# A chunked recurrence on one Trainium2 core: small work moved off VectorE, and a new trace order for output work, late values and the first group's tail

## The chip, the cores and the metric

One core of a Trainium2 chip runs the program. Five engines work beside each other, each on its own stream of instructions: TensorE (PE in the profile, with its weight loads as PEld), VectorE (DVE), ScalarE (ACT), GpSimd (POOL) and SyncE (SP), which here only issues DMAs, in the order of its stream. The metric is the device time of one execution in microseconds; lower is better.

## The reference

One step of a two-layer model: an RWKV-7 time mix with its feed-forward net (FFN), then a latent attention layer with its FFN. Prompt: 512 tokens behind 16 meta tokens; beside it 8 sequences of 4 new tokens, so 560 rows of width 1024. The part that this change touches is the recurrence, for each of 16 heads of width 64, cut from the reference:

```python
def step(s, inp):                       # s: value x key, one per head
    r_t, d_t, k_t, v_t, kk_t, ka_t = inp
    sa = einsum('bhvk,bhk->bhv', s, kk_t)
    s = s * d_t - sa[..., None] * ka_t + v_t[..., None] * k_t
    return s, einsum('bhvk,bhk->bhv', s, r_t)
...
o = groupnorm(o) * lnx_g + lnx_b + bonus * v     # per head
x = x + (o * g) @ wo                             # then x = x + sqrelu_mlp(rmsnorm(x))
```

The 8 new sequences start from states of their own.

## The kernel before

Matrices are fp32 products made from high and low parts in three passes (L326, L337); the low part of a weight, `wlo`, is a subtraction of 128x1024 elements on VectorE (L308), of some late weights on GpSimd.

The recurrence runs in chunks. The 528 prompt rows are 8 chunks of 64 tokens and a tail of 16, to which the 32 rows of the new sequences are added. In a chunk a head needs a unit triangular inverse T of 64x64, the products with the state, and the state's update. The heads are in two groups of four pairs, `st` = 0 and 1; each chunk is worked in two halves of two pairs.

- `inverse(st)`: 31 steps of a multiply and a subtract on VectorE (L637, L638) make the 32x32 inverses; they go to DRAM (`X_D` at L640, a transposed copy `XT_D` at L643). `inverse_tail` does the same in 15 steps for the tail's 16x16 blocks (L660, L661, store L663, loads into `TTt` L667).
- `merge(st)` loads the blocks (L816, L817, L824) and makes 64x64 inverses from them on PE (L839, L847).
- `chunk` (L882 on for its solve): PE multiplies with the chunk's inputs (L886); ScalarE copies the result (`rb`, L888); PE applies T (L892); two evacuations write the solved rows into `SUV`, one by ScalarE (L894), one by the engine that `VA` names for the group (L893); PE makes the state's increment (L912); GpSimd scales the old state (`SL`, L330); VectorE adds both into the next chunk's `SUV` (L920) and again into the next state `Sp` (L922); PE makes the chunk's output (L928, L932).
- `out(p, a, b)` (L1083 on) is one output step for pairs p, p+1 and the rows a to b: means on PE (L1095), centring on VectorE (L1097), squares on ScalarE (L1098), variances on PE (L1102), Ln and Exp on ScalarE (L1103, L1104), scale and bonus on VectorE (L1106, L1107), the gate's product on PE (L1113) with its weights `lg` loaded through a ring of two (L1112), then L1114 and the split in high and low. `wo0` and `wo1` multiply by `wo` and add x; `late_ffn` runs the first 256 rows through the first quarters of the FFN.
- `tail(st)` works the tail chunk, `states(st)` makes the final states: GpSimd masks (`uvm`) and scales (`Sn`) 128x576 elements, PE multiplies (L1042, L1043), VectorE adds.
- `v_late` computes the second group's values, adds them to the bonus (`z`, L1196, stored at L1197) and transposes them into `V_D` (L601 on PE).

What sets the order: `rwkv()` has these as flows, named I (inverse and merge of group 1), J (inverse of the tail), C (chunks of group 0), Y (`v_late`), Oa and Ob (output steps of group 0, first 256 rows and the other 304), L and M (tails of group 0 and 1), W (`wo0`), S and Q (states), D (chunks of group 1), Pa and Pb (output steps of group 1), Xa and Xb (`wo1`), F (`late_ffn`). Each has a list of what must be done before it, and an entry in `PLAN` of a start and a step. A loop takes the flow with the smallest due time among those that may go, runs one piece and adds its step. The order of this trace is a priority for the scheduler that places the instructions on each engine. Needs that matter here: Oa needs C's pieces up to 21 (half of its chunks), L needs C and J, Ob needs L, D needs I and Y, Pa needs D's pieces up to 21 and Ob, M needs D and J, Pb needs M and Pa, F needs Xa, Xb needs Pb and F.

Of the kernel before, what the change touches and what calls it, by code (L numbers as in the profile page):

```python
# [19 lines left out]
D = 1024  # L20
# [12 lines left out]
C = 64  # L33
# [172 lines left out]
class Kern:  # L206
# [3 lines left out]
    ORDER = ["B0 P R D-1 C0 P A1 P E0 P"] * NP  # L210
    WL, ON_V = [1, 4, 6, 8], ((0, 1, 2, 3), (0, 1))
    AMIX, LOP = {4: (0, 1, 2, 3, 4, 5, 6, 7), 5: (0, 1, 2, 3, 4, 5, 6)}, {0: (), 2: (7,)}
    JP, VA, NQ = False, (False, True), (False, False)
    STILL, UNTIL, LATE_LO = (), "I", True
    ON_P, CL = 2, 7
    RA, S0R, MT, VL = 1, True, False, (False, False)
    NPUMP = [0, 0, 0, 2, 4, 4, 4, 4]
    PLAN = dict(I=(0, 1), J=(5.2, 3), C=(6.4, 0.7), Y=(0, 2), Oa=(61, 1.5), L=(72, 1), Ob=(36.5, 0.231), W=(72, 1),
                S=(88.5, 7.65), D=(39, 1), Pa=(74.5, 1), Xa=(70, 0.357), F=(70.5, 0.85), M=(80.5, 0.708), Pb=(85, 1.152), Q=(91.5, 2.309), Xb=(80, 1.7))

    def __init__(self, tc, I, O):
        self.tc, self.nc, self.I, self.O = tc, tc.nc, I, O
# [187 lines left out]
    def rwkv(self):  # L410
        nc, tc, I, O, dr = self.nc, self.tc, self.I, self.O, self.dr
# [4 lines left out]
        halves = (slice(0, 64), slice(64, 128))  # L416
# [46 lines left out]
        V = [self.a(f"V{p}") for p in range(NP // 2)]  # L463
        spans = (slice(0, TA), slice(TA, T))
        for s in spans:
            q = self.sm()
# [105 lines left out]
        for k in range(KT):  # L572
            l = l1[k // 4][:, k % 4, :]
            st = dict(start=(k == 0), stop=(k == KT - 1))
            fw, fa, fg = lm[k]
            for h in range(2):
                hs = slice(h * TH, (h + 1) * TH)
# [276 lines left out]
        def pk(q, n):  # L854
            return q[:, 0:64 * n].rearrange("p (a n) -> p a n", n=64)

        def load_chunk(st, c):
            d = ch[st][c] = {"S": [None, None]}
            ps = slice(4 * st, 4 * st + 4)
            if c < 8:  # L860
                d["W"] = tuple(self.xr(f"W{st}_{c}{i}", [128, 4, 128]) for i in range(2))
                d["V"] = v = self.xr(f"SUV{st}_{c}", [128, 4, 2, 64])
                d["AK"] = self.xr(f"AKc{st}_{c}", [128, 8, 64])
                d["R"] = self.ring("r", f"R{st}_{c}", [128, 4, 64], NP)
            else:
                d["W"] = tuple(self.a(f"Wt{st}{i}", [128, 4, 128]) for i in range(2))
                d["V"] = v = self.a(f"SUVt{st}", [128, 4, 2, 64])
                d["AK"] = self.a(f"AKt{st}", [128, 8, 64])
                d["R"] = self.a(f"Rt{st}", [128, 4, 64])
            for i in range(2):  # L870
                gate[st, c] = nc.sync.dma_start(d["W"][i], W_D[c, :, 8 * st + 4 * i:8 * st + 4 * i + 4, :])
            if self.VL[st]:
                nc.sync.dma_start(v, V_D[c, :, ps, :].unsqueeze(2).to_broadcast([128, 4, 2, 64]))
            else:
                nc.sync.dma_start(v[64:128, :, 0, :], V_D[c, 64:128, ps, :])
                nc.sync.dma_start(v[0:64, :, 1, :], V_D[c, 0:64, ps, :])
            nc.sync.dma_start(d["AK"], AK_D[c, :, 8 * st:8 * st + 8, :])
            nc.sync.dma_start(d["R"], R_D[c, :, ps, :])
# [19 lines left out]
        def alternate(inner, outer, prs):  # L898

            for i, pr in enumerate(prs):  # L900
                first, second = (outer, inner) if i % 2 else (inner, outer)
                first(i, pr, True)
                second(i, pr, False)

        def chunk(st, c, hf):
            d = ch[st][c]
            W, V, AK, R = (d[k] for k in ("W", "V", "AK", "R"))
            Sp = d["S"][hf]
            heads, vs = yield from solve(st, W, V, lambda pr: TT[st][pr][:, c, :], [2 * hf, 2 * hf + 1])
            q = self.sm()  # L910
            for i, pr, par in heads:
                nc.tensor.matmul(q[halves[par], i * 64:i * 64 + 64], AK[:, 2 * pr + par, :], V[:, pr, par, :], start=True, stop=True)  # L912
            SL = self.s("SL")
            p0 = 4 * st + 2 * hf
            self.pmul(SL, Sp, LE[:, p0:p0 + 2, c:c + 1].to_broadcast([128, 2, 64]))
            nxt = ch[st][c + 1]
            if c < 7:
                for par in range(2):
                    hs = halves[par]
                    nc.vector.tensor_add(nxt["V"][hs, vs, par, :], pk(q, 2)[hs], SL[hs])  # L920
            nxt["S"][hf] = self.s("Sp")
            nc.vector.tensor_add(nxt["S"][hf], pk(q, 2), SL)  # L922
            yield
            q = self.sm()

            def inner(i, pr, first):
                for par in range(2):
                    nc.tensor.matmul(q[halves[par], i * 64:i * 64 + 64], V[:, pr, par, :], W[pr // 2][:, 2 * (pr % 2) + par, 64:128], start=first, stop=not first)  # L928

            def outer(i, pr, first):  # L930
                for par in range(2):
                    nc.tensor.matmul(q[halves[par], i * 64:i * 64 + 64], Sp[halves[par], i, :], R[halves[par], pr, :], start=first, stop=not first)  # L932
            alternate(inner, outer, [2 * hf, 2 * hf + 1])
            o = 64 * (c % 4)
            nc.scalar.copy(Of[p0, TA * (c // 4)][:, :, o:o + 64], pk(q, 2))
            yield

        def chunks(st):
# [3 lines left out]
            for hf in range(2):  # L942
                d["S"][hf] = self.s("Sp")
                nc.gpsimd.memset(d["S"][hf], 0.0)
            for par in range(2):
# [112 lines left out]
        nxt = dict(R=self.RA)  # L1058
# [113 lines left out]
        def run(*gens):  # L1172
            for g in gens:
                yield from g
# [26 lines left out]
        def late_ffn():  # L1201
            self.stat_seg(0, TA)
            for q in range(self.EARLY):
                yield from self.ffn_seg(q, 0, TA)
# [3 lines left out]
            I=(run(inverse(1), merge(1)), ()),  # L1208
            J=(inverse_tail(), ()),
            C=(c0, ()),  # L1210
            Y=(v_late(), ()),
            Oa=(run(out(0, 0, TA), out(2, 0, TA)), (("C", 21),)),
            L=(tail(0), ("C", "J")),
            Ob=(run(out(0, TA, T), out(2, TA, T)), ("L",)),
            W=(wo0(), ("Oa", "Ob", "Y", ("D", 1))),
            S=(states(0), ("L",)),
            D=(chunks(1), ("I", "Y")),
            Pa=(run(out(4, 0, TA), out(6, 0, TA)), (("D", 21), "Ob")),
            Xa=(wo1(0, TA), ("Pa", "W")),
            F=(late_ffn(), ("Xa",)),  # L1220
            M=(tail(1), ("D", "J")),
            Pb=(run(out(4, TA, T), out(6, TA, T)), ("M", "Pa")),
            Q=(states(1), ("M",)),
            Xb=(wo1(TA, T), ("Pb", "F")))
        done = {n: 0 for n in flows}
        at = {n: self.PLAN[n][0] for n in flows}
        free, now = set(), 0
# [3 lines left out]
        while flows:  # L1231
# [7 lines left out]
            try:  # L1239
                next(flows[n][0])  # L1240
                done[n] += 1
                at[n] += self.PLAN[n][1]
            except StopIteration:
# [680 lines left out]
```

## Time and profile before

| | us |
|---|---|
| median of 3 runs | 1704.0 (1700.67 to 1707.35) |
| profiled execution | 1705.09, its span 1703.3 |
| PE busy in the span | 1575.3 (92%), mean granted clock 0.952 |
| VectorE busy | 972.1 (57%) |
| ScalarE busy | 667.0 (39%) |
| GpSimd busy | 348.4 (20%) |

The span runs from the first instruction to the last. A busy PE still loses time where its granted clock is below 1.00. The stage that the change concerns runs from about 339 us, where the second group's inverse, the first group's chunks and the late values start together, to about 720 us, where the FFN goes on with all rows.

### The profile page before, as it was taken

The page shows a single profiled execution, that of the slowest core. Times are in us where ns is not written, and L with a number is a line of the kernel's source. Part 1 is how long each engine was busy: PE and PEld are TensorE (multiplying, and loading weights), DVE is VectorE, ACT ScalarE, POOL GpSimd, SP SyncE. Part 2 cuts the span into 40 slices and gives each one's busy share as a digit, 9 for nine tenths or more (in the row PEclk, how much of TensorE's full clock was granted, in tenths as well). Part 3 has the DMA queues.
Part 4 walks back from the last instruction along what each step waited for, and adds up shares of the span by engine and source line. Part 5 has one row for each costly group of instructions (what it writes and reads, how often), then busy time and mean ns, then how long its engine had stood idle before and what let it go on. Part 6 is the DMA issues. An engine that isn't in the chain of part 4 may idle for free.

```text
span 1703.3 us, 33334 instructions
## 1 busy us (share of the span) xinstructions
PE 1575.3 (92%) x13474; PEld 1442.5 (85%) x13474; DVE 972.1 (57%) x1601; ACT 667.0 (39%) x1236; POOL 348.4 (20%) x467
## 2 busy tenths in 40 slices
PE   7699897798899997999999999899999999999996
PEld 6478786686689886999999998767679999999996
DVE  6775678465466677555444656555635444444456
ACT  4374545333445443443331442344534331322222
POOL 3623525442111123000000012773500000000000
PEclk9889897698899998999999999999999999999998
DMA  6334556977834454454232243787612222222223
GB/s 206 128 94 129 181 148 189 256 219 191 241 117 156 158 184 140 137 156 129 87 100 78 86 145 117 230 284 222 190 51 81 91 90 87 88 87 87 87 88 102
DMA packets 156475, 240.04 MB, mean 141 GB/s; under 512 B 68417, under 2 KB 100082, under 8 KB 156322
## 3 DMA queue, kind: packets, MB, share of 16 engines
q1 hardware_dynamic: 140466, 189.59, 36.9%
q0 software_dynamic: 15280, 47.59, 8.5%
q8 instruction: 106, 1.74, 0.4%
q10 hardware_dynamic: 576, 0.74, 0.1%
q14 instruction: 47, 0.39, 0.1%
HBM read 200.50 MB, written 37.37 MB: 140 GB/s over the span
## 4 chain that ended last, share of the span: by engine, by line
PE 54%; DVE 2%; ACT 2%; DMA 1%; issue 1%; SPq 1%; POOL 0%; DVEq 0%; ACTq 0%; POOLq 0%
PE mm L326 31%; PE mm L337 12%; PE sm L337 2%; PE sm L1749 2%; PE sm L1656 1%; PE sm L1700 1%; ACT whi L307 1%; PE sm L1602 1%; DMA lN<-latN,idx 1%; PE sm L1640 0%; DVE wlo L308 0%; PE sm L1703 0%; DMA raw<-wall 0%; DVE y L1861 0%; PE mm L1616 0%
## 5 line engine op out<-in xcount | busy, mean ns | idle before, releaser
L307 ACT CAST whi<-raw 128x1024 fp32r<-128x1024 f32 x218 | 228.8, 1050 | 639.7 <-PE mm L326 356.9
L308 DVE TENSOR_TENSOR wlo<-raw,whi 128x1024 fp32r<-128x1024 f32 x214 | 267.4, 1250 | 280.1 <-ACT whi L307 278.2
L337 PE MATMUL mm<-xs,whi 128*128 128x256 f32 (+1 forms) x1024 | 201.0, 294 | 1.4 <-DVE fd L1316 0.9
L337 PEld LDWEIGHTS mm<-xs,whi 128*128 128x128 f32 x1024 | 163.9, 190 | 2.6 <-issue 1.4
L337 PE MATMUL mm<-xs,wlo 128*128 128x256 f32 (+1 forms) x512 | 149.9, 293 | 0.0
L326 PE MATMUL mm<-hh,wlo 128*128 128x272 f32 (+1 forms) x640 | 133.5, 290 | 0.0
L326 PE MATMUL mm<-hl,whi 128*128 128x272 f32 (+1 forms) x640 | 133.4, 290 | 0.0
L326 PE MATMUL mm<-hh,whi 128*128 128x272 f32 (+1 forms) x640 | 133.3, 290 | 0.0
L326 PE MATMUL mm<-h_ffn,whi 128*128 128x272 f32 x512 | 106.2, 289 | 0.5 <-ACT fr L1350 0.5
L326 PE MATMUL mm<-l_ffn,whi 128*128 128x272 f32 x512 | 105.8, 288 | 0.0
L326 PE MATMUL mm<-h_ffn,wlo 128*128 128x272 f32 x512 | 105.4, 287 | 0.0
L326 PEld LDWEIGHTS mm<-hh,whi 128*128 128x128 f32 x640 | 101.1, 188 | 0.0
L326 PEld LDWEIGHTS mm<-hh,wlo 128*128 128x128 f32 x640 | 100.9, 188 | 0.0
L326 PEld LDWEIGHTS mm<-hl,whi 128*128 128x128 f32 x640 | 100.7, 188 | 0.0
L337 PEld LDWEIGHTS mm<-xs,wlo 128*128 128x128 f32 x512 | 97.1, 190 | 0.1
L1859 POOL TENSOR_TENSOR y<-x,rstd 128x272 f32<-128x272 f32 x4 | 3.5, 895 | 456.6 <-DVE wlo L308 449.7
L337 PE MATMUL mm<-hh,wlo 128*128 128x256 f32 (+1 forms) x256 | 76.2, 298 | 5.0 <-DVE wlo L308 5.0
L326 PEld LDWEIGHTS mm<-h_ffn,whi 128*128 128x128 f32 x512 | 79.9, 188 | 1.0 <-ACT fr L1350 1.0
L326 PEld LDWEIGHTS mm<-l_ffn,whi 128*128 128x128 f32 x512 | 80.2, 188 | 0.0
L326 PEld LDWEIGHTS mm<-h_ffn,wlo 128*128 128x128 f32 x512 | 80.1, 188 | 0.0
L337 PE MATMUL mm<-hl,whi 128*128 128x256 f32 (+1 forms) x256 | 75.8, 296 | 3.0 <-DVE hl L1308 3.0
L337 PE MATMUL mm<-hh,whi 128*128 128x256 f32 (+1 forms) x256 | 76.5, 299 | 0.1
(472 smaller groups left out, 3824.3 us busy)
## 6 DMA issues: line engine op xcount, KB each, us to landing
raw<-wall SPq DMA_DIRECT2D x222, 512.0 KB, 3.6
lT<-latT SPq DMA_DIRECT2D x80, 160.0 KB, 3.6
W_D<-sc POOLq DMA_DIRECT2D x16, 512.0 KB, 3.8
W<-W_D SPq DMA_DIRECT2D x32, 256.0 KB, 4.7
AK_D<-akt SPq DMA_DIRECT2D x8, 576.0 KB, 4.6
s<-state SPq DMA_DIRECT2D x16, 256.0 KB, 3.2
AKc<-AK_D SPq DMA_DIRECT2D x16, 256.0 KB, 4.3
V_D<-vt POOLq DMA_DIRECT2D x8, 288.0 KB, 6.3
```

Source lines behind the costliest of these rows:

```text
L307: nc.scalar.copy(hi, raw)
L308: self.lo_on.tensor_sub(lo, raw, hi.bitcast(F32))
L326: nc.tensor.matmul(v[:, h, :], wt[:, k, :], xt[:, off + h * n: off + (h + 1) * n], start=(first and k == 0 and e == 0), stop=(last and k = ...
L337: self.nc.tensor.matmul(v, wt[:, k, :], xt, start=(k == 0 and e == 0), stop=(k == len(xs) - 1 and e == 2))
L1602: nc.tensor.matmul(o, l[:, k0:k0 + kw], w[:, 2 + k, :], start=(k == 0 and e == 0), stop=(k == 1 and e == 2))
L1656: nc.tensor.matmul(q[:, q0:], V[h // 2][b][:, 128 * (h % 2):128 * (h % 2) + 128], PT[b] if b else Pm[h % 2], start=(b == 0), stop=(b == 4))
L1700: nc.tensor.matmul(q[32 * bb:32 * bb + 32, cols], qlT[:, r, 4 * g + bb, :], lt[bb][:, :, 128 * r + 64 * k:128 * r + 64 * k + 64], start=(r ...
L1749: nc.tensor.matmul(qa[rs, 0:RANK], PT[jp // 2][:, o:o + 32], nat[bb][:, RANK * k:RANK * k + RANK], start=(jp == 0 and k == 0), stop=False)
L1859: nc.gpsimd.tensor_mul(y[:, i], x[m][:, s], r)
```

## The change

Four things. The tail's inverse `J` is computed on GpSimd (`JP`). The first group's solved rows are evacuated by ScalarE twice, the second group's by ScalarE and VectorE (`VA`). For the first group the next state `Sp` is no longer added by VectorE; GpSimd copies it in two halves from the next chunk's `SUV`, which holds the same sum (`SP_P`). And `PLAN` has other numbers. The lines below the edited function stand 6 further down afterwards.

```diff
@@ -210,13 +210,14 @@
     ORDER = ["B0 P R D-1 C0 P A1 P E0 P"] * NP
     WL, ON_V = [1, 4, 6, 8], ((0, 1, 2, 3), (0, 1))
     AMIX, LOP = {4: (0, 1, 2, 3, 4, 5, 6, 7), 5: (0, 1, 2, 3, 4, 5, 6)}, {0: (), 2: (7,)}
-    JP, VA, NQ = False, (False, True), (False, False)
+    JP, VA, NQ = True, (True, False), (False, False)
+    SP_P = (True, False)
     STILL, UNTIL, LATE_LO = (), "I", True
     ON_P, CL = 2, 7
     RA, S0R, MT, VL = 1, True, False, (False, False)
     NPUMP = [0, 0, 0, 2, 4, 4, 4, 4]
-    PLAN = dict(I=(0, 1), J=(5.2, 3), C=(6.4, 0.7), Y=(0, 2), Oa=(61, 1.5), L=(72, 1), Ob=(36.5, 0.231), W=(72, 1),
-                S=(88.5, 7.65), D=(39, 1), Pa=(74.5, 1), Xa=(70, 0.357), F=(70.5, 0.85), M=(80.5, 0.708), Pb=(85, 1.152), Q=(91.5, 2.309), Xb=(80, 1.7))
+    PLAN = dict(I=(0, 1), J=(0, 1), C=(6.4, 0.7), Y=(0, 1.3), Oa=(33, 1.5), L=(36, 1), Ob=(36.5, 0.5), W=(42, 2),
+                S=(78.5, 7.65), D=(38, 1), Pa=(64.5, 1), Xa=(70, 0.357), F=(70.5, 0.85), M=(72.5, 0.708), Pb=(85, 1.152), Q=(91.5, 2.309), Xb=(80, 1.7))
 
     def __init__(self, tc, I, O):
         self.tc, self.nc, self.I, self.O = tc, tc.nc, I, O
@@ -914,13 +915,18 @@
             p0 = 4 * st + 2 * hf
             self.pmul(SL, Sp, LE[:, p0:p0 + 2, c:c + 1].to_broadcast([128, 2, 64]))
             nxt = ch[st][c + 1]
+            nxt["S"][hf] = self.s("Sp")
             if c < 7:
                 for par in range(2):
                     hs = halves[par]
                     nc.vector.tensor_add(nxt["V"][hs, vs, par, :], pk(q, 2)[hs], SL[hs])
-            nxt["S"][hf] = self.s("Sp")
-            nc.vector.tensor_add(nxt["S"][hf], pk(q, 2), SL)
-            yield
+            if c < 7 and self.SP_P[st]:
+                for par in range(2):
+                    hs = halves[par]
+                    nc.gpsimd.tensor_copy(nxt["S"][hf][hs], nxt["V"][hs, vs, par, :])
+            yield
+            if c == 7 or not self.SP_P[st]:
+                nc.vector.tensor_add(nxt["S"][hf], pk(q, 2), SL)
             q = self.sm()
 
             def inner(i, pr, first):
```

With the new numbers the trace has `Y` done before the last chunks of `C`, `Oa` and `L` around the end of `C` instead of behind `D`, `Ob` and `W` beside `D`, `Pa` and `Xa` earlier, and `Pb` behind the last piece of `F`, where it had been between the pieces.

SP, where the loads for the second group's chunks are issued, before: behind the merge's loads (`TT`) stand the bonus load and store (`z`, L1193, L1197), the tail inverse's store and loads (L663, L667), then the first chunk's `SUV`.

```order
L824 DMA TT_4303<-X_D_120 32x8x32 x4
L1193 DMA z_4581<-BV_D 128x560
L878 DMA R_3_4823<-R_D 128x256
L1197 DMA BV_D<-z_4581 128x560
L1090 DMA bv_0_4807<-BV_D 128x256
L1090 DMA bv_0_4808<-BV_D 128x256
L663 DMA X_D<-X_3364 48x256
L1090 DMA bv_0_4922<-BV_D 128x256
L1090 DMA bv_0_4923<-BV_D 128x256
L667 DMA TTt<-X_D 16x8x16 x4
L875 DMA SUV_0_4619<-V_D 64x4x64
```

The same place afterwards:

```order
L825 DMA TT_4436<-X_D_120 32x8x32 x4
L1096 DMA bv_0_4473<-BV_D 128x256
L1096 DMA bv_0_4474<-BV_D 128x256
L876 DMA SUV_0_4731<-V_D 64x4x64
L877 DMA SUV_0_4731<-V_D 64x4x64
L878 DMA AKc_0_4732<-AK_D 128x512
L872 DMA W_10_4740<-W_D 128x512
L872 DMA W_11_4741<-W_D 128x512
L876 DMA SUV_1_4742<-V_D 64x4x64
L877 DMA SUV_1_4742<-V_D 64x4x64
L878 DMA AKc_1_4743<-AK_D 128x512
L1118 DMA lg_0_4810<-lorag 128x128
```

The bonus's and the tail inverse's DMAs are gone from between the merge's loads and the first `SUV`; the gate's weights for an output step now follow the second chunk's loads.

PE at the start of the second group's chunks, before: the late values' last transposes (L601), one output step, the first chunk.

```order
L601 MATMUL sm<-cst,V_4580 128x128 x8
L601 MATMUL sm<-cst,V_4580 64x128
L1102 MATMUL mm<-sqo,cst 128x256 x2
L1113 MATMUL mm<-hg,lg_0_4890 128x256
L1113 MATMUL mm<-hg,lg_0_4893 128x256
L1095 MATMUL mm<-Of_0_3407,cst 128x256 x2
L886 MATMUL sm<-SUV_0_4619,W_00_4617 64x64
L886 MATMUL sm<-SUV_0_4619,W_01_4618 64x64
L886 MATMUL sm<-SUV_0_4619,W_00_4617 64x64 x3
L886 MATMUL sm<-SUV_0_4619,W_01_4618 64x64 x3
L892 MATMUL sm<-rb,TT_4300 64x64 x2
L892 MATMUL sm<-rb,TT_4301 64x64 x2
```

Afterwards (L1005 and L1108 to L1119 are the tail and the second output step, then the tail's and the first chunk's solves):

```order
L1005 MATMUL sm<-QRt,Sp 64x32 x8
L1108 MATMUL mm<-sqo,cst 128x256 x2
L1119 MATMUL mm<-hg,lg_0_4810 128x256
L1119 MATMUL mm<-hg,lg_0_4813 128x256
L887 MATMUL sm<-SUVt_4375,Wt_4373 64x64
L887 MATMUL sm<-SUVt_4375,Wt_4374 64x64
L887 MATMUL sm<-SUVt_4375,Wt_4373 64x64 x3
L887 MATMUL sm<-SUVt_4375,Wt_4374 64x64 x3
L893 MATMUL sm<-rb,TTt 64x64 x8
L887 MATMUL sm<-SUV_0_4731,W_00_4729 64x64 x4
L887 MATMUL sm<-SUV_0_4731,W_01_4730 64x64 x4
L893 MATMUL sm<-rb,TT_4433 64x64 x2
```

The transposes are no longer there; the tail of the first group and the second output step stand ahead of the first chunk.

PE at the last output steps of the second group, before, with the matmuls of the FFN piece (L337) around them:

```order
L337 MATMUL mm<-hh,whi_6999 128x256
L337 MATMUL mm<-hl,whi_6999 128x256
L337 MATMUL mm<-hh,wlo_7000 128x256
L1102 MATMUL mm<-sqo,cst 128x304 x2
L337 MATMUL mm<-hh,whi_7029 128x256
L337 MATMUL mm<-hl,whi_7029 128x256
L337 MATMUL mm<-hh,wlo_7030 128x256
L337 MATMUL mm<-hh,whi_7029 128x256
```

Afterwards, behind the last matmul of the FFN pieces (row one):

```order
L338 MATMUL mm<-hh,wlo_7109 128x256
L1108 MATMUL mm<-sqo,cst 128x304 x2
L1119 MATMUL mm<-hg,lg_256_7210 128x304
L1119 MATMUL mm<-hg,lg_256_7213 128x304
L1048 MATMUL sm<-uvm,AKt_4376 64x512
L1049 MATMUL sm<-uvm,AKt_4376 64x64
L1048 MATMUL sm<-uvm,AKt_4376 64x512
L1049 MATMUL sm<-uvm,AKt_4376 64x64
L1101 MATMUL mm<-Of_4_5461,cst 128x304 x2
L1108 MATMUL mm<-sqo,cst 128x304 x2
L1119 MATMUL mm<-hg,lg_256_7244 128x304
L1119 MATMUL mm<-hg,lg_256_7247 128x304
```

Two output steps and the states' matmuls (L1048, L1049) now follow each other with no FFN matmul between them.

## Rows read from the trace of the kernel before

**Rows 1.** Windows; columns: stretch, length, busy us of PE, PEld, DVE, ACT, POOL, clock, DMA.

```profile
339.00:408.30 69.30, 67.20 (x908) 56.55 (x906) 50.23 (x151) 25.54 (x78) 28.99 (x52) 1.00 0.79 228
408.30:438.30 30.00, 19.77 (x323) 15.75 (x323) 9.76 (x28) 10.19 (x26) 4.05 (x11) 0.66 0.61 140
438.30:461.00 22.70, 19.41 (x382) 16.25 (x382) 12.85 (x44) 11.54 (x40) 3.37 (x8) 0.92 0.94 257
461.00:530.00 69.00, 67.16 (x652) 57.62 (x650) 45.29 (x101) 32.41 (x73) 6.99 (x14) 1.00 0.46 146
530.00:641.90 111.90, 109.84 (x891) 99.79 (x892) 76.51 (x98) 49.03 (x67) 25.83 (x30) 1.00 0.52 168
641.90:652.30 10.40, 5.37 (x28) 5.16 (x27) 6.61 (x5) 1.05 (x1) 3.51 (x4) 0.67 0.38 118
652.30:676.30 24.00, 18.87 (x120) 15.35 (x118) 21.53 (x36) 11.68 (x21) 7.06 (x8) 0.98 0.46 147
```

**Rows 2.** Timeline of PE; columns: start, length, engine, line, operation, [idle before <-releaser].

```profile
412.46 0.24 PE L839 MATMUL sm<-xt,n 32*32 32x32 f32 x2 [4.20 <-DMA xt<-XT_D]
440.41 0.64 PE L886 MATMUL sm<-SUV,W 128*64 128x64 f32 x16
444.50 0.64 PE L886 MATMUL sm<-SUV,W 128*64 128x64 f32 x16
452.20 1.13 PE L1113 MATMUL mm<-hg,lg 128*128 128x256 f32 x4 [2.05 <-DMA lg<-lorag]
647.23 0.58 PE L337 MATMUL mm<-hh,wlo 128*128 128x256 f32 x1 [5.03 <-DVE wlo L308]
```

**Rows 3.** Timeline of SP's DMA queue, 413 to 433 us.

```profile
413.17 8.03 SPq L824 DMA_DIRECT2D TT<-X_D  x14
425.28 0.32 SPq L1197 DMA_DIRECT2D BV_D<-z  x1
428.37 0.33 SPq L663 DMA_DIRECT2D X_D<-X  x1
432.20 0.59 SPq L875 DMA_DIRECT2D SUV<-V_D  x1
```

**Rows 4.** Groups by line, 330 to 640 us: count | busy, mean ns | idle before.

```profile
L922 DVE TENSOR_TENSOR Sp<-sm,SL 128x128 f32<-128x128 f32 x32 | 9.3, 291 | 2.8 <-PE sm L912 2.2
L893 DVE TENSOR_SCALAR SUV<-sm 64x128 f32<-64x128 f32 x16 | 4.4, 279 | 5.1 <-PE sm L892 5.1
L661 DVE TENSOR_TENSOR X<-X,itmp 48x15 f32<-48x15 f32 (+7 forms) x15 | 3.7, 247 | 0.2
L990 POOL COPY Wt<-SQ 64x64 f32<-64x64 f32 x8 | 2.6, 320 | 22.7 <-DMA Wt<-W_D 20.9 <-DMA AKt<-AK_D 1.7
```

**Rows 5.** Timeline of POOL and DVE, where both read SBUF.

```profile
371.84 2.36 POOL L308 TENSOR_TENSOR wlo<-raw,whi 128x1024 fp32r<-128x1024 f32 x1
364.29 0.42 DVE L638 TENSOR_TENSOR X<-X,itmp 128x247 f32<-128x247 f32 x1
371.94 2.54 DVE L638 TENSOR_TENSOR X<-X,itmp 128x247 f32<-128x247 f32 x1
640.47 5.56 DVE L1318 TENSOR_TENSOR x<-x,fd 128x256 f32<-128x256 f32 x2
667.28 3.72 DVE L308 TENSOR_TENSOR wlo<-raw,whi 128x1024 fp32r<-128x1024 f32 x1
```

**Rows 6.** Groups by line and shape, 330 to 680 us: output step, states.

```profile
L1102 PE MATMUL mm<-sqo,cst 128*128 128x304 f32 x16 | 5.0, 432 | 0.0
L1103 ACT ACTIVATE sqo<-mm,eps 128x608 f32<-128x608 f32 x4 | 3.1, 769 | 1.5 <-PE mm L1102 1.4
L1106 DVE SCALAR_TENSOR_TENSOR cen<-cen,vecs,sqo 128x304 f32<-128x304 f32 x8 | 3.9, 530 | 4.3 <-ACT sqo L1104 4.3
L1114 DVE TENSOR_TENSOR cen<-mm,cen 128x608 f32<-128x608 f32 x4 | 3.1, 784 | 0.1
L330 POOL TENSOR_TENSOR uvm<-SUVt,cst 128x576 f32<-128x576 f32 x16 | 19.6, 1248 | 34.3 <-DVE x L1318 27.8 <-issue 4.9 <-PE sm L1023 1.6
```

## Prediction

> **What bounds the kernel now.** I read the windows of the stage first, one for each change in what runs [rows 1]: a stretch's length less PE's busy time times the granted clock is what PE loses there, by idling or at the lower clock. A change that leaves PE's instructions as they are (this one does) can only win back such loss, or add to it. In order the seven stretches lose 2.1, 16.95, 4.84, 1.84, 2.06, 6.8 and 5.5 us, 40.1 in all. In the first, where the first group's chunks, the second inverse and the late values run together, VectorE is busy 50.23 of 69.3 us, but PE 67.20 at full clock: PE is the bound. The big hole is 408.3 to 461, with 21.8 us: the end of the inverse, its merge and the start of the second group's chunks. The next are 641.9 to 652.3 and the stretch behind it, 12.3 us.
>
> Then the timelines say what ends the waits. In the hole PE first waits 4.20 us for the transposed inverse, later 2.05 us for gate weights [rows 2]. On SP's queue the merge's fourteen loads end at 413.17 + 8.03 = 421.2; the store of `z` goes at 425.28, the tail inverse's store at 428.37, and only at 432.20 the first load of `SUV` for the second group [rows 3]. The two in between wait for VectorE's results, and everything behind them on SP waits too. At 647.23 PE has idled 5.03 us for a VectorE split [rows 2], which stood behind two additions that took 5.56 us together beside GpSimd's `uvm` [rows 5, 6].
>
> The mean granted clock of 0.66 and 0.67 in the two holes (2.4 GHz is 1.00, the lower level 1.2 GHz) follows the idling there, and is 1.00 in the dense stretches [rows 1].
>
> **The change, part by part.** The sum is made against the profiled execution: 1705.1 us, its span 1703.3 and 1.8 around it. That is 1.1 above the median of three, 1704.0, well inside their spread.
>
> *Tail inverse, copies, evacuations.* VectorE loses 30 operations of the tail inverse (its subtractions 247 ns [rows 4]; the multiplies I take at 0.2 to 0.25), 14 state additions of 291 ns and, in the first group, 16 evacuations of 279 ns [rows 4]: 7 + 4.1 + 4.5, about 15 us. The evacuations come back to VectorE in the second group, where it is busy 45.29 of 69.0 us [rows 1] while PE is full; ScalarE has the same count. GpSimd gains 30 operations and 28 copies; the nearest row is its copy of 64x64, 320 ns [rows 4], so 58 x 0.32 = 18.6 us on top of 28.99 in 69.3 [rows 1], which fits. The cover for all of it is PE, busy 67.2 of 69.3 us. The late values' last transposes, about 2.6 us of PE work that filled part of the hole before, now lie in this stretch: its end moves back by that and the 4.20 us wait shrinks by as much, so that is nil too. For the inverse, the true start of the hole, 15 us less beside it would be a gain, and GpSimd's reads beside it a loss. Between an inverse earlier by the 2.1 us that PE loses there and one later by 6 (below) I take 0.
>
> Here rule and row bear on a loss. The same subtraction of 128x247 took 0.42 us alone and 2.54 while GpSimd made a `wlo` of 2.36 us beside it [rows 5]. The Trainium skill, "SBUF — State Buffer", section "Who interferes with whom", says that a VectorE instruction with two inputs in SBUF and a GpSimd instruction that reads SBUF share a port pair, and whichever comes second is blocked until the first ends. The trace agrees. By that rule in full each of the 58 new GpSimd operations would hold back an inverse step, which is the fourth case below; by the row of the first window alone the cost is nil.
>
> *The hole.* Two trace edits act here. The late values and the tail's inverse end early, so their DMAs no longer stand between the merge's loads and `SUV`: the first `SUV` load can go at about 422, 10 us earlier. But PE is not simply 10 us earlier, because its order now has the second output step and the tail's solve ahead of the first chunk, and that output step's gate weights stand on SP behind the loads of two chunks. SP needs about 0.6 us a load [rows 3], so ten loads behind 422 are issued by 428; with a landing of 2 to 3 us the gate's product starts at about 431. The tail's solve and the first chunk's follow, each about 1.6 us, and VectorE's part of the output step between them: the chunk's state product comes at about 438, as before. What is gained is the work that is done by then and was done later before: the tail, some 40 small matmuls by the chunk's cadence of 4.09 us (440.41 to 444.50 [rows 2]) for 80 of them, 2.05; one pair of gate products 0.9; the wait of 2.05 for gate weights, which no longer falls between chunks; and the clock there, (1 - 0.92) x 19.41 = 1.55 [rows 1]. Together 6.5. Bounds: 0 if SP's later loads or ScalarE, which now has both evacuations' neighbours and the output step, are late again; 12 if the first chunk does run from 430, which would leave 10 of 21.8.
>
> *Output work beside the second chunks.* PE loses 1.84 us in 69 there [rows 1]. Moving `Oa`, `Ob`, `W` in or out of a stretch that PE fills changes the order, not the length: 0. The FFN pieces (530 to 641.9, 2.06 lost) the same.
>
> *The last output steps.* Before, `Pb` lay between the FFN pieces. Now two steps follow each other behind the last piece. One step's chain behind its statistics is 0.43 (PE) + 2 x 0.77 (ScalarE) + 4 x 0.53 + 0.78 (VectorE) = 4.9 us [rows 6]; the second step's begins with its own centring and square, about 1.6, so two take 11.4. PE has in that time ten matmuls of 0.432 and three pairs of the states' (by columns 0.82 a pair): 6.8. It idles 4.6, and by the clock of the earlier hole, 0.67 on 5.37 us [rows 1], loses 1.8 more: 6.4. The 6.8 of 641.9 to 652.3 would go, as the FFN additions there no longer meet four `uvm` in a row. But the states' GpSimd work of 16 x 1.25 us [rows 6] now lies beside `wo1`, whose additions and splits are VectorE's: where two `uvm` met a split, it took 3.72 us, about 2.5 of it waiting [rows 5]. I take one and a half such meetings, 3.8. Net 6.4 + 3.8 - 6.8 = 3.4 dearer. Bounds: -6.8 (all hidden) and +13 (third case below).
>
> *Sum:* 1705.1 + 0 - 6.5 + 0 + 3.4 = 1702.0 us.
>
> **The rivals.**
>
> *Second case, SP was the bound of the hole.* For it: everything behind 421.2 on SP waited for VectorE [rows 3]. If the gate weights and the output step come through quickly, the hole keeps only the wait for the inverse and one output step's latency, about 10 of 21.8, and the last steps cost no more than the 6.8 that go. That is 1705.1 - 11.8 = 1693.3. Against it: the order of PE itself, with two dependent chains ahead of the first chunk.
>
> *Third case, slower: the last output steps lie bare.* With no FFN matmul behind `Pb`, both chains are served one after the other, also queued on VectorE behind the late splits, and four `uvm` meetings instead of one and a half: idle 9, clock 3, 4 x 2.5 = 10, less 6.8, so +15.2; the hole gives back 5. The time is 1715.3. It decides from the point where PE idles over 10 us between the last FFN piece and the FFN with all rows. For it speaks 647.23, where one VectorE delay became 5.03 us idle and the low clock [rows 2]. Against it: the second step can overlap the first.
>
> *Fourth case, GpSimd holds the inverse back.* All 58 operations block an inverse step for their 0.32 us: 18.6 less the 12.5 us of VectorE work that the inverse no longer has beside it (its share of the 15) is 6 later, and the hole starts later by that: 1708. Against it: GpSimd's operations are short and not all meet one.
>
> That the relief of VectorE does nothing is part of the forecast; that nothing at all moves would be 1705.
>
> **How the numbers follow.** About 0.5%, 8.5 us, can be told from no change. Forecast 0.42, second case 0.30, third 0.22, fourth 0.06. The forecast's own range is 1697 to 1708, all of it within 0.5% of 1704. Of the fourth case half lies within it and half, with some of the third's costs, above. Faster: 0.30 and 0.01 from the forecast's lower end. Slower: 0.22 and 0.03. Same: 0.44. The range reaches to the middle of the outer cases with their spreads, 1688 to 1717, leaving out about 1 in 10 on either side.
>
> **What will show it.** On SP the first `SUV` of the second group should load at about 422, and PE's first state product of that group should still start at 436 to 440. The FFN's first statistics matmul (530 before) should come at about 523. Behind the last FFN piece there should be PE idle of 4 to 6 us in the output steps and a clock under 0.9 in that stretch, and no 5 us wait for `wlo` in the pieces. In the first stretch PE should be as dense as before, with the inverse's store within 2 us of 404. If the first state product comes near 430, the second case holds; if the idle time behind the pieces is above 10 us, the third; if the inverse ends at 408 or later, the fourth.

## Result and profile after

The kernel became slower: 1726.01 us in the median (1721.23 to 1727.57, 4 runs) against 1705.67 for the kernel before beside it; the ratio is 1.0112, its 95% interval 1.0071 to 1.0153. The profiled execution took 1726.61 us, its span 1724.9, 21.6 more than before. The forecast was 1702.0, no change, with a range of 1688 to 1717: the time lies above it.

Five moments cut the two spans into stages that can be compared: the first step of the second inverse on VectorE, its transposed copy (which ends it), PE's first state product of the second group's chunks, the first statistics matmul of the FFN pieces and the second one, for all other rows.

| stage, us | before | after | more |
|---|---|---|---|
| to the first step | 348.15 | 347.27 | -0.9 |
| second inverse | 53.8 | 59.9 | 6.1 |
| to the first state product | 36.4 | 44.2 | 7.9 |
| second group's chunks, to the FFN pieces | 91.7 | 89.8 | -1.9 |
| FFN pieces and last output steps | 146.3 | 153.7 | 7.4 |
| to the end | 1027.0 | 1030.1 | 3.1 |

They sum to 21.7; the difference to 21.6 is rounding. Each comes from one execution; those of the changed kernel lie 6 us apart, so that a stage's 2 or 3 us alone prove little. Windows of the four middle stages, before; columns are stretch, length, busy us of PE, its weight loads, VectorE, ScalarE and GpSimd, granted clock, DMA share, GB/s:

```profile
348.15:401.91 53.76, 51.89 (x724) 43.35 (x722) 44.67 (x136) 19.78 (x60) 20.12 (x37) 1.00 0.83 236
401.91:438.28 36.37, 25.91 (x419) 20.38 (x415) 13.63 (x40) 12.37 (x34) 6.42 (x18) 0.72 0.63 157
438.28:530.02 91.74, 86.59 (x1029) 73.89 (x1029) 58.16 (x144) 43.95 (x113) 10.36 (x22) 0.98 0.58 174
530.02:676.28 146.26, 134.06 (x1035) 120.29 (x1035) 104.62 (x137) 61.76 (x89) 36.40 (x41) 0.97 0.50 161
```

The same four after:

```profile
347.27:407.13 59.86, 53.30 (x688) 44.61 (x688) 37.53 (x91) 25.24 (x78) 36.23 (x89) 0.96 0.76 226
407.13:451.38 44.25, 31.32 (x538) 25.62 (x539) 15.33 (x40) 15.27 (x44) 6.45 (x22) 0.69 0.77 205
451.38:541.17 89.79, 86.74 (x948) 72.84 (x946) 55.51 (x141) 36.41 (x90) 9.03 (x16) 0.97 0.37 114
541.17:694.82 153.65, 133.84 (x1018) 119.28 (x1019) 100.82 (x136) 61.11 (x86) 34.27 (x39) 0.96 0.50 159
```

PE's busy time in the first is about the same. VectorE is busy 37.5 us there instead of 44.7, though the stage is longer: it waits more. In the second stage PE's busy time rises by 5.4 us at a granted clock of 0.69: matmuls that were moved there, and low clock. The second group's chunks, the only one of the four that gained, have 1.9 us to show for it. In the last PE does the same 134 us of work in 7.4 us more.

Timeline of PE after, its long waits:

```profile
403.85 1.36 PE L887 MATMUL sm<-SUV,W 128*64 128x64 f32 x9 [3.39 <-issue]
...
433.09 0.31 PE L848 MATMUL sm<-TT,zs 32*32 32x32 f32 x2 [7.02 <-ACT zs L843]
...
447.92 1.12 PE L893 MATMUL sm<-rb,TT 64*64 64x64 f32 x16 [5.40 <-ACT rb L889]
...
647.64 1.53 PE L1108 MATMUL mm<-sqo,cst 128*128 128x304 f32 x4 [2.43 <-ACT sqo L1104]
656.97 1.29 PE L1108 MATMUL mm<-sqo,cst 128*128 128x304 f32 x4 [3.02 <-ACT sqo L1104]
...
671.84 0.41 PE L338 MATMUL mm<-oo,wlo 128*128 128x304 f32 x1 [2.20 <-DVE wlo L309]
...
694.82 1.38 PE L1291 MATMUL mm<-acc,cst 128*128 128x304 f32 x2 [6.89 <-DVE acc L1170]
```

Before, the waits behind the inverse were 4.20 us [rows 2], 3.17 for the squares of an output step, which [rows 2] leaves out, and 2.05 for gate weights, which came behind the first state product [rows 2]; the last row below is the wait ahead of the second statistics matmul:

```profile
429.84 2.07 PE L1102 MATMUL mm<-sqo,cst 128*128 128x256 f32 x4 [3.17 <-ACT sqo L1098]
...
676.28 1.38 PE L1285 MATMUL mm<-acc,cst 128*128 128x304 f32 x2 [5.13 <-DVE acc L1164]
```

Now they are 7.02 and 5.40, with one of 3.39 ahead of the inverse's end. The wait of 5.03 for `wlo` among the FFN pieces [rows 2] is gone as forecast, and in its place, among the output steps and behind them, stand 2.43, 3.02 and 2.20. The last wait, for `acc`, grew from 5.13 to 6.89.

The chain of waits of the stretch from 420 to 452 us after says what stood behind the two longest (start, length, what):

```profile
427.39 2.52 DMA bv<-BV_D
...
430.99 0.70 DVE cen L1120
...
432.45 0.59 ACT zs L843
...
433.70 1.91 PE sm L848 x62
...
440.06 5.39 DMA bv<-BV_D
445.55 0.50 DVE cen L1113
446.14 0.70 DVE cen L1120
447.18 0.40 ACT oo L375
447.92 1.12 PE sm L893 x16
```

What is shown starts at a DMA, which stood on SP behind the merge's loads: the bonus `bv` of a first-group output step. VectorE's addition L1113 waits for it; then L1120; then ScalarE, whose cast of that output step stands ahead of `zs` (L843), which the merge needs; then PE (L848). Then it repeats: the second step's bonus, VectorE, ScalarE's cast ahead of `rb`, and PE's apply of the first chunk (L893). Timeline after of VectorE, the wait ahead of the first of those additions and an earlier one, and of ScalarE, the cast that had waited 7.96 us:

```profile
402.64 0.74 DVE L1202 TENSOR_TENSOR z<-mm,z 128x560 f32<-128x560 f32 x1 [5.72 <-DMA z<-BV_D]
...
403.48 0.60 DVE L922 TENSOR_TENSOR SUV<-sm,SL 64x128 f32<-64x128 f32 x2
...
430.00 0.88 DVE L1113 SCALAR_TENSOR_TENSOR cen<-cen,vecs,bv 128x256 f32<-128x256 f32 x2 [5.34 <-DMA bv<-BV_D]
...
431.71 0.71 ACT L375 CAST oo<-cen 128x256 fp32r<-128x256 f32 x2 [7.96 <-DVE cen L1120]
```

SP after shows why the loads are late. The first step's bonus loads are issued at 427.39, behind the merge's fourteen loads that take 9.69 us (8.03 before [rows 3]). The second step's are issued at 439.59, behind the loads of the first chunks, and one of them then takes 5.39 us to land. The first `SUV` follows at 428.36, 3.8 us earlier than before [rows 3] and not 10.

```profile
395.36 0.42 SPq L305 DMA_DIRECT2D raw<-wall  x1
395.88 0.38 SPq L1199 DMA_DIRECT2D z<-BV_D  x1
...
417.59 9.69 SPq L825 DMA_DIRECT2D TT<-X_D  x14
427.39 0.86 SPq L1096 DMA_DIRECT2D bv<-BV_D  x2
428.36 0.59 SPq L876 DMA_DIRECT2D SUV<-V_D  x1
...
439.59 0.86 SPq L1096 DMA_DIRECT2D bv<-BV_D  x2
```

The earlier one is the wait ahead of L1202 (the late value's multiply by its bonus) at 402.64, for `z` of the last late value, issued at 395.88 behind a weight load. A state addition of the first group (L922, 403.48) and the last inverse steps stand behind it on VectorE. PE has nothing to do for 3.39 us and starts at 403.85, with the products of `SUV`. The profile names nothing that it waited for ("issue"); that it was this addition, which writes `SUV`, is read from the times alone. In the stretch behind it PE is full for 16 us and granted half. Below are that stretch and two in which PE makes the same 80 matmuls of one half of a chunk, once at full clock and once at half:

```profile
404.00:420.00 16.00, 15.95 (x175) 12.59 (x177) 5.88 (x18) 5.89 (x21) 8.39 (x29) 0.50 0.82 212
...
396.00:400.47 4.47, 4.43 (x81) 3.52 (x80) 0.85 (x3) 2.27 (x10) 2.33 (x6) 1.00 0.93 259
413.84:420.00 6.16, 6.16 (x85) 5.31 (x86) 1.24 (x4) 2.34 (x9) 3.45 (x12) 0.51 0.84 157
```

At 0.50 (1.2 GHz) instead of 1.00 (2.4 GHz) the same work takes 1.7 of 6.16 us longer, not twice as long. By that the 16 us hold about 4.4 us of loss (an estimate), behind an idle time of 3.39 that was the longest since the stage began.

The waits of VectorE inside the second inverse, from its first step to its transposed copy, by groups, before and after (count, busy, mean ns, idle before and what ended it):

```profile
L1196 DVE TENSOR_TENSOR z<-mm,z 128x560 f32<-128x560 f32 x3 | 2.2, 731 | 0.0
...
L1202 DVE TENSOR_TENSOR z<-mm,z 128x560 f32<-128x560 f32 x4 | 3.0, 742 | 11.3 <-DMA z<-BV_D 10.0 <-ACT V L1201 1.3
```

The 62 inverse steps themselves were busy 26.8 us, against 28.1 before.

In the last output steps the second step's statistics (656.97) wait for its squares on ScalarE, these for its centring on VectorE (L1103), and that stands behind the first step's bonus addition (L1113), in order of engines ScalarE, VectorE:

```profile
656.20 0.71 ACT L1104 ACTIVATE sqo<-cen 128x608 f32<-128x608 f32 x1 [5.42 <-DVE cen L1103]
...
653.54 1.86 DVE L1113 SCALAR_TENSOR_TENSOR cen<-cen,vecs,bv 128x304 f32<-128x304 f32 x2
655.33 0.84 DVE L1103 SCALAR_TENSOR_TENSOR cen<-mm,Of 128x304 f32<-128x304 f32 x2
...
686.95 4.54 DVE L1170 TENSOR_TENSOR acc<-acc,psq 128x304 f32<-128x304 f32 x1
```

The last row is an addition to `acc` that takes 0.46 us elsewhere; beside it GpSimd made `Sn` and two `uvm`. From the last matmul of the FFN pieces (645.21) to the second statistics matmul PE idles 16.7 of 49.6 us, the 6.89 included.

### The profile page after: what moved, and what is told of

The parts are those of the page before. It is cut to its first block, busy times and chain, and to the rows that moved or that the text cites. A ratio compares the mean times of both kernels' runs of the same rounds, so it can differ in the third digit from the quotient of the medians.

```text
span 1724.9 us, 33338 instructions
## 1 busy us (share of the span) xinstructions
PE 1587.6 (92%) x13474; PEld 1449.8 (84%) x13474; DVE 963.0 (56%) x1557; ACT 666.9 (39%) x1236; POOL 369.4 (21%) x525
## 4 chain that ended last, share of the span: by engine, by line
PE 73%; DVE 11%; DMA 6%; ACT 4%; issue 3%; SPq 2%; POOL 1%; DVEq 0%; ACTq 0%; POOLq 0%
PE mm L327 37%; PE mm L338 18%; DMA raw<-wall 3%; PE sm L338 2%; DVE wlo L309 2%; PE sm L1755 2%; ACT whi L308 1%; PE sm L775 1%; PE sm L1662 1%; DVE itmp L638 1%; PE sm L913 1%; PE sm L938 1%; PE sm L934 1%; DMA lT<-latT,pidx 1%; PE sm L1608 1%
```

## Experiments

A ratio is to the kernel before, run beside it on the same chip; 95% intervals in brackets. The first four ran on a chip on which the kernel before took 1704.9 us, the others on three on which it took 1749 to 1751 (in the kernels traced there, what is longer lies behind the FFN's second statistics matmul). So expectations in us are read as ratios to 1705 there, and stage times are compared instead of spans.

**The engine moves alone.**

```diff
-    PLAN = (numbers of after)
+    PLAN = (numbers of before)
```

> The three moves of small work (tail inverse to GpSimd, evacuations swapped, state copied by GpSimd) with the plan's numbers of before. Theory A (the loss comes from the new trace order: on VectorE's in-order stream a bonus addition waits for a load that SP issues behind the merge's loads, and ScalarE and PE wait behind it): no difference from before, 1700 to 1710 us, inverse of the second group stored within 2 us of before. Theory B (GpSimd's reads hold VectorE's inverse back): 6 us or more slower, 1710 to 1716, inverse stored 4 us later.

1.0032 [1.0005, 1.0059], 1709.78 us: at the upper end of theory A's range, but the interval leaves out 1, so it is a small loss. The inverse was 50.6 us, 3.2 shorter than before (theory A had it within 2), so GpSimd's work did not lengthen it. Its 62 steps were busy 29.8 us against 28.1 before, so about 1.7 us is all that GpSimd's short operations can have cost them here, and VectorE's relief outweighed it. But PE's first merge matmul was no earlier (412.46 before [rows 2]):

```profile
415.54 0.28 PE L840 MATMUL sm<-xt,n 32*32 32x32 f32 x2 [3.79 <-DMA xt<-XT_D]
```

SP of that kernel issues the transposed inverse's store at once and then stands at an `R` load and sixteen `TT` loads, before the `xt` that PE waits for:

```profile
399.41 0.49 SPq L644 DMA_DIRECT2D XT_D<-XT  x1
402.01 0.31 SPq L879 DMA_DIRECT2D R<-R_D  x1
402.87 9.02 SPq L825 DMA_DIRECT2D TT<-X_D  x16
412.95 0.44 SPq L818 DMA_DIRECT2D xt<-XT_D  x1
```

What VectorE gained was lost in a queue.

**The plan alone.**

```diff
-    JP, VA, NQ = True, (True, False), (False, False)
-    SP_P = (True, False)
+    JP, VA, NQ = False, (False, True), (False, False)
+    SP_P = (False, False)
```

> The plan's new numbers alone, the small work on the engines of before. Theory A: about all of the loss, 1720 to 1730 us, with PE waits of 5 us and more at the merge and at the second group's first chunk. Theory B: less than 12 us of the 20, under 1718.

1.012 [1.0091, 1.0148], 1722.01 us: the whole loss, as theory A says. (In this kernel, as in the other versions on this code, the state addition of the second group and, without `SP_P`, of the first stands one trace step later than before; with the plan of before that made no difference, see the moves one at a time.) The inverse took 60.9 us. Its longest wait on VectorE is here 5.33 us for a load of the early tail inverse, and only 1.70 for `z`. The pattern in the hole is there without any engine move; VectorE and then PE of this kernel:

```profile
427.69 0.88 DVE L1113 SCALAR_TENSOR_TENSOR cen<-cen,vecs,bv 128x256 f32<-128x256 f32 x2 [5.16 <-DMA bv<-BV_D]
```

```profile
430.77 0.31 PE L848 MATMUL sm<-TT,zs 32*32 32x32 f32 x2 [5.23 <-ACT zs L843]
444.76 1.28 PE L893 MATMUL sm<-rb,TT 64*64 64x64 f32 x16 [4.90 <-ACT rb L889]
```

**Bonus loads on another queue.**

```diff
-                    nc.sync.dma_start(bv[i][:, :n], BV_D[p + i, :, a:b])
+                    (nc.gpsimd if a == 0 and p < 4 else nc.sync).dma_start(bv[i][:, :n], BV_D[p + i, :, a:b])
```

> The changed kernel, but the four bonus loads of the first group's early output steps go on GpSimd's DMA queue and so no longer stand behind the merge's loads on SP. Theory A: the PE waits of 7.02 and 5.40 us shrink below 2 us each and some low clock goes with them: 8 to 14 us back, 1712 to 1718, start of the FFN pieces at 527 to 533. Theory C (the hole is long because the second group's inverse ends 3.5 us later and the merge's loads take longer): the waits go elsewhere, under 3 us back, 1723 or more.

1.0096 [1.0079, 1.0113], 1720.25 us, between the two theories. The two waits went as theory A says, and the FFN pieces began at 530.7 (541.2 after, 530.0 before): from the inverse's end 126.6 us later (134.0 after, 128.1 before). Its PE timeline:

```profile
423.99 1.07 PE L848 MATMUL sm<-TT,zs 32*32 32x32 f32 x32 [0.91 <-DMA TT<-X_D]
433.10 2.05 PE L1119 MATMUL mm<-hg,lg 128*128 128x256 f32 x4 [3.41 <-DMA lg<-lorag]
439.30 0.68 PE L893 MATMUL sm<-rb,TT 64*64 64x64 f32 x16 [0.94 <-ACT rb L889]
```

In their place is one of 3.41 us for gate weights, which the forecast had put there. The time fell by less than expected: 5.8 us between medians, and as a ratio the interval overlaps that of the changed kernel, so this run alone doesn't settle the size.

**Last output steps between the FFN pieces.**

```diff
-F=(70.5, 0.85), M=(72.5, 0.708), Pb=(85, 1.152)
+F=(70.5, 1.3), M=(72.5, 0.708), Pb=(83, 1.152)
```

> The changed kernel, with the last output steps of the second group traced between the FFN pieces again (start 83 and not 85, the pieces' step 1.3 and not 0.85). Theory A: the bare output steps cost what the stretch from the FFN's first statistics to its second grew by, 7.5 us: 1716 to 1721. Rival D (the growth there is GpSimd's states work against VectorE, wherever the output steps stand): 1723 or more.

1.0072 [1.0054, 1.009], 1715.92 us, 10 us between medians. The stage from the first to the second statistics matmul is 147.0 us (153.7 after, 146.3 before), and what followed it 1026.9 (1030.1 after). The waits among the output steps are gone; what is left is the states' `uvm`, and the wait for `acc` that was 5.13 before too. Rival D falls as it was put, since the growth does not come wherever the output steps stand. But part of it in the changed kernel is GpSimd's states work against VectorE: the addition of 4.54 us.

```profile
671.96 1.07 PE L1048 MATMUL sm<-uvm,AKt 128*64 128x512 f32 x2 [2.30 <-POOL uvm L331]
681.37 1.38 PE L1291 MATMUL mm<-acc,cst 128*128 128x304 f32 x2 [5.13 <-DVE acc L1170]
```

**Both mends together** (the two diffs above).

> The changed kernel with both mends: the four bonus loads on GpSimd's queue and the last output steps between the FFN pieces. If the two losses are separate stretches (theory A), the gains add, about 6 and 10 us off 1726: 1707 to 1713. If they are one loss that is only put off (rival), no better than the better of the two: 1714 or more.

1.0014 [0.9987, 1.0041]: no difference from before that can be measured, within theory A's 1.001 to 1.005, and clear of the intervals of either mend alone. The inverse still took 58.0 us; from its end to the FFN pieces 125.8 (134.0 after, 128.1 before), the pieces 146.2. So these two account for nearly all the loss. How it divides between them is not settled: in the stretch from the inverse's end to the FFN pieces the bonus loads take off 7.5 us alone (134.0 to 126.6) and 4.2 beside the other mend (130.0 to 125.8).

**And `z` on GpSimd's queue too.**

```diff
-                nc.sync.dma_start(z[:, :T], BV_D[p])
+                nc.gpsimd.dma_start(z[:, :T], BV_D[p])
```

> As the one with both mends, and the late values' bonus loads (z) on GpSimd's queue as well. Theory A: the wait of 5.72 us on VectorE for the last z, which held back a state addition and the inverse and after which PE ran about 15 us at half clock, goes: 4 to 8 us less than the kernel with both mends, 1701 to 1707. Rival: the z load is late because the DMA engines are busy and not because of its place on SP, or stands behind the tail inverse on GpSimd: no gain over the kernel with both mends.

1.0063 [1.004, 1.0086]: no gain, rather worse, as the rival says. The last `z` no longer waits, and yet the inverse took 60.8 us: other waits stand in its place, the longest 6.36 us of VectorE for a state product, ahead of which PE had the late values' matmuls, and 6.16 for the first `z`. So the price of the last `z` wait by itself stays open, and that it lengthens the inverse is not shown.

**Moves alone, xt loads first**, and then **the tail's inverse early as well.**

```diff
-                    nc.sync.dma_start(ac(xt[i][o:o + 32]), ...)
+                    last = nc.sync.dma_start(ac(xt[i][o:o + 32]), ...)
...
+                            with tc.issue_after(last.ins):
```

```diff
-J=(5.2, 3)
+J=(0, 1)
```

> Engine moves alone with the plan of before, and the merge's sixteen TT loads are issued behind its xt loads. Theory A: with the moves alone the inverse ended 3 us sooner after its start, but the xt loads stood behind the sixteen TT loads, so the merge began no earlier; with xt first PE's first merge matmul comes at 406 to 409 and the time is 1700 to 1706. Theory B (the moves cost by GpSimd's reads): as with the moves alone, 1708 to 1712.

> As the last, and the tail's inverse is traced early (start 0, step 1), so that its store and loads no longer stand ahead of the second group's first SUV on SP. Theory A: that SUV loads 4 to 8 us earlier; 1694 to 1702, under before. Rival: the first chunk then waits for the late z or for the output step on VectorE instead, 1703 or more.

1.0036 [1.0014, 1.0059] and 1.0043 [1.0024, 1.0062]. Both of theory A's expectations missed. In the first SP stood 5.11 us at two `R` loads ahead of the merge's loads, and the `xt` were again issued only at 412: mending one place in the queue brought the next to the front. In the second the inverse took 59.3 us (50.7 in the first). Its longest wait on VectorE is 8.67 us (5.06) for a state product of PE, which stood behind the late values' matmuls; how the early tail inverse brings that order about is open.

**The moves one at a time**, with the plan of before: the evacuations, the tail's inverse, the state copies.

```diff
+    JP, VA, NQ = False, (True, False), (False, False)
+    SP_P = (False, False)
...
+    JP, VA, NQ = True, (False, True), (False, False)
+    SP_P = (False, False)
...
+    JP, VA, NQ = False, (False, True), (False, False)
+    SP_P = (True, False)
```

> Of the three engine moves the evacuations alone, with the plan of before. Theory S (the moves' 0.3% comes from the load order on SP that they bring): within 0.2% of before, since the merge's xt loads still stand ahead of most TT loads. Theory V (from the second group's evacuation on VectorE, for which PE waited 1.48 and 1.05 us with the moves alone): 0.2 to 0.4% slower, all of the moves' loss.

> The tail's inverse on GpSimd alone, with the plan of before. Theory S: within 0.2% of before, load order on SP nearly as before. Theory B (GpSimd's reads hold VectorE's inverse back): the second inverse takes longer than 53.8 us, 0.2% or more slower.

> The state copies on GpSimd alone, with the plan of before. Theory S: six TT loads now stand ahead of the merge's xt loads on SP; 0.2 to 0.4% slower, first merge matmul on PE 2 us or more later. Theory V: within 0.2% of before.

1.0011 [0.9992, 1.0029], 1.0001 [0.9987, 1.0016] and 0.998 [0.9964, 0.9996]. None has the 0.3% that the three have together, so neither theory S nor V holds: the first two make no difference that can be told, and the copies alone gain 0.2%, against the expectation. With the tail's inverse alone on GpSimd the second inverse took 54.5 us, 0.7 longer: theory B's sign, without its loss. With the copies alone it took 51.0 us. What else they gain can't be read from their trace: that execution took 1749.84 us, the second-longest of its ten and no faster than before's median there. A wait of PE at a `z` is in it again:

```profile
396.39 2.07 PE L1101 MATMUL mm<-Of,cst 128*128 128x256 f32 x4 [3.17 <-DVE z L1202]
```

The gain is small, its interval ends just under 1, and it is the only move that has one by itself.

**Both mends, evacuations as before.**

```diff
-    JP, VA, NQ = True, (True, False), (False, False)
+    JP, VA, NQ = True, (False, True), (False, False)
```

> The changed kernel with both mends (bonus loads on GpSimd's queue, last output steps between the FFN pieces) and the evacuations as before, ScalarE and VectorE in the first group, ScalarE alone in the second. Theory V: 0.2 to 0.4% better than with both mends, ratio to before 0.997 to 1.000. Theory S: no better than with both mends, 1.000 to 1.004.

1.007 [1.0046, 1.0094], worse than both mends, against theory V. The second inverse took 64.8 us (58.0). VectorE is busy 41.2 us in it (37.1), as it has the first group's evacuations again, and PE waits for them five times, 2.8 us in all; the longest:

```profile
395.72 1.20 PE L913 MATMUL sm<-SUV,AKc 128*64 128x64 f32 x15 [1.18 <-DVE SUV L894]
```

So one of the moves, the evacuations, does pay, but only beside the new plan; with the plan of before it made no difference.

**Both mends, late values at the old pace.**

```diff
-Y=(0, 1.3)
+Y=(0, 2)
```

> Both mends, and the late values traced at the pace of before (step 2 and not 1.3). Theory Y (the early late values lengthen the second inverse, 58 to 60 us instead of 53.8, because their z multiplies wait for loads on VectorE's in-order stream): the inverse takes 50 to 54 us again and the last late value's matmuls lie in the merge's hole; ratio to before 0.994 to 0.999. Rival: what the inverse gains the second group's chunks lose, since they need the last late value; ratio 1.001 or more.

1.0154 [1.0116, 1.0193], the slowest of all. The inverse took 50.3 us with nothing but the pace changed, so beside this plan the early late values are what lengthened it. PE has less to do in that stage too (44.4 us busy against 52.9). But the rival's half is the larger: the second group needs the last late value. From the inverse's end to the FFN pieces it took 140.3 us (125.8 with both mends), PE busy 58.2 of the last 68.3, and from there to the second statistics matmul 165.5 (146.2); why this second part grew was not traced.

**State copies alone, bonus loads on GpSimd's queue**, with the plan of before.

```diff
+    JP, VA, NQ = False, (False, True), (False, False)
+    SP_P = (True, False)
...
+                    (nc.gpsimd if a == 0 and p < 4 else nc.sync).dma_start(bv[i][:, :n], BV_D[p + i, :, a:b])
```

> The plan of before, with the state copies on GpSimd alone and the four early bonus loads of the first group on GpSimd's queue. Theory A: SP has four loads less between the late z and the second group's first SUV, about 2 us: ratio to before 0.996 to 0.998, better than the copies alone. Rival: the second group's start waits for z or the output step whatever SP holds: as the copies alone, 0.998 to 1.000.

0.9979 [0.9958, 1.0]: as the copies alone. With the plan of before those four loads cost nothing. This and the copies alone are the versions that came out ahead of both kernels, by 0.2% and, among this many versions, at the edge of what was measured.

## Why the prediction was wrong

*What bounds the kernel now.* Right in the stretches; the hole behind the second inverse and the end of the FFN pieces are where the time changed. The measure of loss, length less busy time times clock, counts work at 0.50 as half lost; by the same 80 matmuls at both clocks 1.7 of 6.16 us are. And [rows 2] lacks the hole's wait of 3.17 us for an output step's squares: an output step already ended a wait there.

*Tail inverse, copies, evacuations: 0, with -2.1 and +6 as bounds.* The inverse took 6.1 us longer, at the edge of the bounds and not for the bound's reason. Its store came at 409.1, past the 408 that was to show the fourth case; yet with the moves alone the inverse was 3.2 us shorter and with the plan alone 7.1 longer, so the sign could not tell GpSimd's reads from the plan. The rule of the Trainium skill ("SBUF — State Buffer", "Who interferes with whom") stands for the long instructions [rows 5]; counted in full for these short ones it gave 6 us that no run shows: the steps' own busy time went from 28.1 to 26.8 us, and to 29.8 with the moves alone. What failed here is "the cover is PE". I took the first stretch as bound by PE because PE was busy 67.2 of 69.3 us. With the new plan VectorE waits between the inverse's steps, 10.0 us of it for the loads of `z` where it had waited nothing, and PE has gaps. With the late values at the old pace the inverse is back at 50.3 us, so their pace is the cause beside this plan. By which of the waits they lengthen it is not shown: without the wait for the last `z` the inverse was as long. And with the plan of before an early tail inverse lengthened it too (59.3), at the old pace of the late values.

*The hole: -6.5, bounds 0 and -12.* The failed step, outside its bounds: from the inverse's end to the FFN pieces it was 134.0 us against 128.1, +5.9. The step is "the chunk's state product comes at about 438, as before". It came at 451.4; 5.2 us of the delay are the inverse's later end, 7.9 arose in the hole; the FFN pieces began at 541.2 and not at 523. I followed SP's queue to the gate weights and stopped there. The bonus loads ahead of them, two issues that I counted, feed a VectorE addition; behind that addition stand VectorE's own merge copies and, through the cast, ScalarE's `zs` and `rb`. So an output step put into a gap made the merge and the first chunk, which bound the gap, wait for its slowest load. I had named "VectorE's part of the output step between" without its price. The mend on the bonus loads and the chain of waits show it. The gain side was partly right: the chunks themselves ran 1.9 us shorter.

*Output work beside the second chunks: 0.* Right within that 1.9.

*The last output steps: +3.4, up to +13.* The mechanism was right and the size was off: 7.4 us up to the second statistics matmul and 3.1 behind it, of which the mend took back 6.6 and 3.2. I let the second step overlap the first, 4.6 us of idle time in all; but its statistics waited 3.02 for its own squares (656.97), as its centring stood on VectorE behind the first step's bonus addition. And the wait for `acc` ahead of 694.82 rose from 5.13 to 6.89, behind the addition of 4.54 us beside GpSimd. The third case had both, and its sign came, PE idle over 10 us (16.7); its +15.2 (the bound of +13 should have been the same figure) was too much, and what it lacked was the hole. Of the 3.1 us the trace shows a part: behind that matmul now stand 16 matmuls of the states, 4.1 us of PE, and before none. That they are all of it is not shown: with the steps between the pieces 8 of them, 2.7 us, stand there without growth, and the three kernels with one move each, traced on one chip, differ by 5 us in this stage (1070.5 to 1075.5).

*The second case* (SP as the bound) had the right queue and the wrong sign: `SUV` did load earlier, and nothing came of it.

## What to carry to other kernels

Work put into a gap brings its waits along. For each moved step follow its slowest operand to the in-order engine that waits for it, and list what stands behind that instruction there; if that is the work the gap waits for, the gap grows. A stretch that is dense because filler is spread over it need not be bound by the engine that is busy: ask what it looks like when the filler comes first. And choose a sign that tells a case from its rivals: the inverse's late end could not.

## What the runs showed of the hardware

After 3.39 us without work PE was granted half clock for a stretch of 16 us in which it was busy 15.95. The same small matmuls took 6.16 us there and 4.47 at full clock, so the idle time cost 3.4 us and the clock behind it about 4.4, an estimate from these rows. With the last output steps between the FFN pieces the same wait was 1.77 us, ahead of 401.02, and from 408 on the granted clock was 1.00 again. In a dense stage a short wait has to be priced with the clock behind it.
